# A hybrid S5 and Conformer layer on one core: inputs laid out by the host, and the modulation product in float32

## The chip, the core and the metric

The kernel runs on one core of a Trainium2 chip. The metric is the device time of one execution in microseconds (us). Five engines work beside each other: PE (TensorE, matrix products into PSUM banks), DVE (VectorE), ACT (ScalarE), POOL (GpSimd) and SP (SyncE, which here only issues transfers). Transfers run on 16 DMA engines that all queues share. PE's clock has two levels in the profile, 1.2 and 2.4 GHz, shown as a granted clock of 0.5 and 1.0.

## What is computed

One layer over 2048 latent tokens and 256 context tokens of width 1024, all in float32. The part that the change touches, cut from the reference:

```python
mod_l = silu_c @ ada_w[i] + ada_b[i]           # six vectors of 1024: shift, scale, gate, twice
mod_c = silu_cc @ ada_w[i] + ada_b[i]
nl = modulate(rmsnorm(h_lat, norm1_g[i]), sh1, sc1)    # h * (1 + scale) + shift
nc = modulate(rmsnorm(h_ctx, norm1_g[i]), csh1, csc1)
zl = nl @ w_in[i]                              # 3584 columns: S5 input 512, conv input 1024, gates 2048
zc = nc @ w_in[i][:, :D_S5]
ys_l, _ = s5_mixer(zl[..., :D_S5], zc[..., :D_S5], ...)
```

Behind it come the S5 scans, a Conformer convolution branch, a gated merge, an output product, a gated MLP with a 3x3 convolution, and a last norm. None of that is changed.

## The kernel before

A product of two float32 matrices is made from three reduced products: `split` writes an operand as a high part (cast) and a low part (source minus high part), and `mm3` (lines 487 to 489) issues high by high, high by low and low by high. `gemm` does so for eight slices of 128 rows of the contraction: 24 matmuls into one PSUM bank.

**Order of work.** The Python code gives a program order. A planner puts each engine's instructions in an order of its own from that order, with `urgent()` moving a block 300 places ahead, and hands out buffers. On the chip each engine, and each queue of transfers, runs its list strictly in order.

**Buffers.** Three tags matter: `t16` (six buffers of 16 KB a partition), `z8` (eight of 8 KB) and `raw` (three of 2 KB for weights). PSUM has four banks under `mm` and four under `ax`.

**Phase 1, first part (about 0 to 48 us), `consts` and `ada_first`.** Vectors are loaded as rows and turned into columns on PE (`columns`, line 580). The first 2048 columns of `ada_w` come as eight slabs of 1 MB. Each slab is split (L474, L476 and L478 with tile `slhl`), and PE multiplies both parts by the split, activated condition vectors `sc4` (L662, four columns; 64 matmuls of 512 columns). The result rows go to `adarow` (a `z8` buffer), are turned into columns (L673) and become scale `A1` and shift `S1`.

**Phase 1, second part (about 48 to 207 us), the S5 input `u`.** Tokens are taken in halves of 256 rows, nine in all. For each half: load `x2` with tokens on partitions, squares on ACT (L711), `rstd` (L501 to L506, with a power on POOL), scaling by token (`scaled`, L718), 16 transposes of 128x128 on PE (`turned`, L728) with copies back on ACT (L729), then `modulate`: scale and shift per channel (L737), high part (L739), low part (L741, half of them on POOL). The products with the first 512 columns of `w_in` run per column block `m`: context and the first 512 tokens in pieces of 256 columns, the other blocks in pieces of 512. `u_out` (L746) puts each result into `ub` and stores it (L749). The modulated tokens `nl[0..3]` stay on chip for the rest of `w_in`; `nl[0..2]` are in `t16`, `nl[3]` is four `z8` buffers.

In between, three background pieces run: `s5_params` (loads in small pieces, transposes, about 110 small DVE operations), `taps` and `taps2` (turn the convolution weights, build a banded table and store it to `d_ct`), and `s5_tables` (32 groups; L267, L268 and L271 on POOL, L269, L270 and L272 on DVE, L273 to L275 on ACT, one store each). 24 of the 32 tables are issued before the part ends.

**Phase 2 (about 214 to 892 us).** 88 products of 512 columns for convolution input and gates. After each, `background()` takes three steps of the S5 work in program order: the tables that are left, `s5_ops` (L301 to L345, with L313 to L317 on POOL) and `s5_main` (L371 to L432, one group of five steps at a time, its products at L391, L392 and L407), and steps of the convolution (L895). Everything behind it is dominated by PE.

## Time and profile before

| | us |
|---|---|
| median of 3 runs | 2859.3 |
| lowest and highest | 2857.84, 2859.38 |
| profiled execution | 2868.82 |
| its span, first to last instruction | 2867.0 |

The profile is one execution. Its span leaves 1.8 us of the execution outside. The granted clock is 0.976 over the span. A busy share is time in which an engine had an instruction in work; matmuls are pipelined, so the distance between two starts, not the length of one, is the price of a matmul in a row of many.

### The profile page before, as it was taken

Reading aid. Unit: us, or ns where it says so; the run is one execution under the profiler, and the core shown is the slowest. Engines: PE = TensorE matmul, PEld = TensorE weight load, DVE = VectorE, ACT = ScalarE, POOL = GpSimd, SP = SyncE. Lnnn points to the kernel's source line nnn. Section 1 sums busy time; section 2 is a strip of 40 time slices with the busy share of each in tenths; the row PEclk is TensorE's granted clock in tenths of the full one; section 3 lists DMA queues with packets and bytes.
Section 4 is the critical chain, followed back from the end, with each engine's and each line's share of the span. In section 5 each row is a group of like instructions: output and inputs, shape, how many; then the busy total and the mean of one; then the engine's idle time right before and its main releaser. Section 6 shows DMA issues by size and latency. Waiting matters only on the chain.

```text
span 2867.0 us, 32800 instructions
## 1 busy us (share of the span) xinstructions
PE 2736.4 (95%) x12286; PEld 2233.3 (78%) x12286; DVE 1539.0 (54%) x2363; ACT 840.1 (29%) x1487; POOL 491.1 (17%) x522
## 2 busy tenths in 40 slices
PE   6879999999999999999999999999999989999998
PEld 3767777878787777788888888888888878787887
DVE  7967633333313688666765565565564653414154
ACT  4554421212123544334422122122222222212122
POOL 3446556666610000000000000000000000000000
PEclk8989999999999999999999999999999999999999
DMA  7434635444444666533211111111111144224143
GB/s 254 124 95 149 203 117 161 148 139 148 155 122 137 199 202 191 198 125 132 81 48 46 54 44 48 56 45 44 59 41 48 57 143 135 96 85 133 46 143 102
DMA packets 341421, 326.44 MB, mean 114 GB/s; under 512 B 110306, under 2 KB 255828, under 8 KB 339725
## 3 DMA queue, kind: packets, MB, share of 16 engines
q1 hardware_dynamic: 255101, 225.76, 26.3%
q10 hardware_dynamic: 86160, 98.57, 9.8%
q8 instruction: 97, 1.59, 0.2%
q14 instruction: 63, 0.52, 0.1%
HBM read 221.01 MB, written 103.24 MB: 113 GB/s over the span
## 4 chain that ended last, share of the span: by engine, by line
PE 70%; DVE 11%; DMA 6%; POOL 5%; issue 4%; ACT 3%; SPq 1%; POOLq 0%; ACTq 0%; DVEq 0%
PE ps L487 22%; PE ps L489 22%; PE ps L488 22%; DMA sgab<-d_sg 2%; PE ps L895 1%; PE ps L407 1%; DVE x L737 1%; DVE Hs L430 1%; DMA w_raw<-in_ffn_w_down_dram 1%; DVE tab L269 1%; POOL t L416 1%; POOL t L417 1%; DVE Hs L432 1%; DMA ada<-in_ada_w_dram 0%; POOL t L383 0%
## 5 line engine op out<-in xcount | busy, mean ns | idle before, releaser
L1342 DVE SCALAR_TENSOR_TENSOR acc<-pad,fw,acc 128x1024 f32<-128x1024 f32 x352 | 450.6, 1283 | 238.9 <-ACT acc L1338 229.5
L502 POOL TENSOR_TENSOR rs_y<-rs_v,mhalf 128x1 f32<-128x1 f32 (+1 forms) x41 | 26.2, 638 | 2065.2 <-DVE rs_v L501 2064.9
L487 PE MATMUL ps<-wd,hhl 128*128 128x512 f32 x704 | 276.1, 393 | 16.1 <-ACT hhl L474 9.5
L488 PE MATMUL ps<-wd,hhl 128*128 128x512 f32 x704 | 276.2, 393 | 0.0
L489 PE MATMUL ps<-wd,hhl 128*128 128x512 f32 x704 | 275.6, 392 | 0.0
L430 DVE TENSOR_TENSOR_SCAN Hs<-m,S 64x287 f32<-64x287 f32 x64 | 68.7, 1074 | 245.1 <-POOL S L418 244.5
L478 DVE TENSOR_TENSOR hhl<-hr,hhl 128x512 fp32r<-128x512 f32 (+1 forms) x110 | 63.0, 583 | 246.7 <-ACT hhl L474 246.7
L478 DVE TENSOR_TENSOR w_ch<-w_raw,w_ch 128x512 fp32r<-128x512 f32 x134 | 99.7, 748 | 142.9 <-ACT w_ch L474 142.6
L487 PEld LDWEIGHTS ps<-wd,hhl 128*128 128x128 f32 x704 | 133.5, 190 | 46.2 <-ACT hhl L474 9.9
L474 ACT CAST w_ch<-w_raw 128x512 fp32r<-128x512 f32 x142 | 87.3, 621 | 246.2 <-PE ps L489 165.6
L488 PEld LDWEIGHTS ps<-wd,hhl 128*128 128x128 f32 x704 | 133.4, 190 | 28.7 <-DVE wd L478 1.1
L489 PEld LDWEIGHTS ps<-wd,hhl 128*128 128x128 f32 x704 | 133.5, 190 | 27.9 <-DVE hhl L478 0.2
L474 ACT CAST hhl<-hr 128x512 fp32r<-128x512 f32 (+1 forms) x110 | 57.2, 534 | 267.2 <-PE ps L489 228.3
L487 PE MATMUL ps<-nm0h,w_ch 128*128 128x512 f32 x344 | 133.8, 389 | 0.0
L488 PE MATMUL ps<-nm0l,w_ch 128*128 128x512 f32 x344 | 133.8, 389 | 0.0
L489 PE MATMUL ps<-nm0h,w_ch 128*128 128x512 f32 x344 | 133.8, 389 | 0.0
L487 PE MATMUL ps<-nm1h,w_ch 128*128 128x512 f32 x344 | 133.8, 389 | 0.0
L488 PE MATMUL ps<-nm1l,w_ch 128*128 128x512 f32 x344 | 133.8, 389 | 0.0
L489 PE MATMUL ps<-nm1h,w_ch 128*128 128x512 f32 x344 | 133.8, 389 | 0.0
L487 PE MATMUL ps<-nm2h,w_ch 128*128 128x512 f32 x344 | 133.8, 389 | 0.0
L488 PE MATMUL ps<-nm2l,w_ch 128*128 128x512 f32 x344 | 133.8, 389 | 0.0
L489 PE MATMUL ps<-nm2h,w_ch 128*128 128x512 f32 x344 | 133.8, 389 | 0.0
(409 smaller groups left out, 6538.8 us busy)
## 6 DMA issues: line engine op xcount, KB each, us to landing
w_raw<-in_ffn_w_up_dram SPq DMA_DIRECT2D x88, 256.0 KB
d_hid<-acc ACTq DMA_DIRECT2D x88, 256.0 KB
w_raw<-in_ffn_w_down_dram SPq DMA_DIRECT2D x76, 256.0 KB
grp<-d_rec SPq DMA_DIRECT2D x32, 576.0 KB
hr<-d_hid SPq DMA_DIRECT2D x66, 256.0 KB
d_sg<-sgg ACTq DMA_DIRECT2D x64, 256.0 KB
ada<-in_ada_w_dram SPq DMA_DIRECT2D x64, 256.0 KB
sgab<-d_sg SPq DMA_DIRECT2D x32, 512.0 KB
```

Of the source, the lines that this page charges most:

```text
L269: v.scalar_tensor_tensor(tt, idx, h, tk, op0=OP.mult, op1=OP.subtract)
L407: nc.tensor.matmul(ps[:, :NX], sm[:, i, :], ug, start=True, stop=True)
L416: g_.tensor_tensor(t1, S, tb[:, 0:1, :].to_broadcast([128, 2, NX]), op=OP.mult)
L417: g_.tensor_tensor(t2, S[:, ::-1, :], tb[:, 1:2, :].to_broadcast([128, 2, NX]), op=OP.mult)
L430: v.tensor_tensor_scan(Hs[0:64, i, 1:1 + nsc], mb[0:64], S[0:64, i, 0:nsc], 0.0, op0=OP.mult, op1=OP.add)
L432: v.tensor_tensor_scan(Hs[64:128, i, NX - 1 - nsc:NX - 1][:, ::-1], mb[64:128], S[64:128, i, NX - nsc:NX][:, ::-1], 0.0, op0=OP.mult, op1= ...
L474: self.a.copy(hi, src)
L478: e.tensor_tensor(lo, src, hi.bitcast(F32), op=OP.subtract)
L487: mm(ps, wh, xh, start=first, stop=False)
L488: mm(ps, wh, xl, start=False, stop=False)
L489: mm(ps, wl, xh, start=False, stop=last)
L1342: v.scalar_tensor_tensor(acc[:, h], win(h, t // 3, t % 3), fw[:, i, t:t + 1], acc[:, h], op0=OP.mult, op1=OP.add)
```

## The change

The host hands in further copies of inputs, laid out as the core wants them: `xt` and `ctxt` (tokens with channels on partitions), `cols` (all per-channel vectors as columns), `fdw` and `ct` (the convolution weights, the banded table finished), and the S5 parameters with the state on partitions. `x` and `ctx` in their old form are still loaded, now for the squares alone.

- `columns`, `taps`, `taps2`, `turned`, `scaled` and the transposes in `s5_params` are gone. `xt` is loaded as raw slabs, `xt[b, q]`, two `z8` buffers for each block of 512 tokens.
- `ada_first` multiplies the slabs as they are: 32 matmuls in float32, two columns, no split.
- The reciprocal root of all tokens is collected in `rms`. `row` makes from it a PSUM bank that holds it along the tokens on all partitions: a diagonal matrix on DVE and a float32 product with ones, per 128 tokens.
- Context and block 0 are scaled by token as soon as they are there (`early`) and modulated later (`late`). Blocks 1 to 3 use `modulate`: one DVE operation multiplies by scale and by the token row (read from PSUM), ACT adds the shift and writes the high part, one DVE operation writes the low part. POOL takes a quarter of the low parts in `late`, none in `modulate`.
- The products run by pairs of column blocks with the contraction outermost, in pieces of 512 columns for block 0 too.
- 18 of the 32 tables are issued before the part ends: 3, 6 and 9 behind blocks 1, 2 and 3.

```diff
+        cols = cp.tile([128, NCOL + 32], F32, name="cols")
+        self.dma(cols[:, :NCOL], ins["cols"])
...
         for k in range(8):
-            sl = self.z8("slab", [128, 2048])
-            self.dma(sl, self.ins["ada_w"][128 * k:128 * k + 128, 0:2048])
-            hl = self.t16("slhl", [128, 2, 2048])
-            for h in range(2):
-                hs = slice(1024 * h, 1024 * h + 1024)
+            if k % 2 == 0:
+                sl = self.t16("slab", [128, 2, 2048], F32)
+            self.dma(sl[:, k % 2], self.ins["ada_w"][128 * k:128 * k + 128, 0:2048])
+            for j in range(4):
                 with self.urgent():
-                    self.split(hl[:, 0, hs], hl[:, 1, hs], sl[:, hs], "va"[h], "g" if h and k in (0,2,4) else "v")
-                for i in range(2):
-                    for j in (2 * h, 2 * h + 1):
-                        pe.matmul(acc[j][:4, :], self.sc4[:, k, :], hl[:, i, 512 * j:512 * j + 512],
-                                  start=(k == 0 and i == 0), stop=(k == 7 and i == 1))
+                    pe.matmul(acc[j][:2, :], self.sc[:, k, :], sl[:, k % 2, 512 * j:512 * j + 512],
+                              start=(k == 0), stop=(k == 7))
...
+            def half_stats(i):
                 x2 = self.z8("x2", [128, 2, D])
+                src = ins["x"][256 * i:256 * i + 256, :] if i < 8 else ins["ctx"]
                 self.dma(x2, src.rearrange("(j p) d -> p j d", p=128))
                 ss = small.tile([128, 2], F32, name="nt_ss")
                 for j in range(2):
+                    a.activation(x2[:, j, :], x2[:, j, :], AF.Square, accum_out=ss[:, j:j + 1])
+                self.rstd(small, ss, 2, 1.0 / D, rms[:, 2 * i:2 * i + 2])
+            def row(i, n):
+                ps = psum.tile([128, 512], F32, name="ps", tag="ax")
+                for j in range(n // 128):
+                    dg = small.tile([128, 128], F32, name="dg")
+                    v.tensor_scalar(dg, self.ident, rms[:, 2 * i + j:2 * i + j + 1], None, op0=OP.mult)
+                    self.pe.matmul(ps[:, 128 * j:128 * j + 128], self.ones, dg, start=True, stop=True)
+                return ps
+            def raw_block(b):
+                for q in range(2):
+                    t = self.z8("xt", [128, 4, 512])
+                    self.dma(t, ins["xt"][b][:, 4 * q:4 * q + 4])
+                    xt[b, q] = t
...
+            def modulate(b):
+                nl[b] = self.nl_tiles(b, "nl")
+                for k in range(8):
+                    hi, lo = nl[b](0, k), nl[b](1, k)
+                    w, s1 = xt[b, k // 4][:, k % 4], self.S1[:, 0, k:k + 1]
+                    v.scalar_tensor_tensor(w, w, self.A1[:, 0, k:k + 1], srow[b], op0=OP.mult, op1=OP.mult)
+                    a.activation(hi, w, AF.Identity, bias=s1)
+                    v.scalar_tensor_tensor(lo, w, s1, hi.bitcast(F32), op0=OP.add, op1=OP.subtract)
...
+                if k == 7:
+                    for m in range(2):
+                        wu[m] = self.wtile(ring, w_in, 128 * m)
+                    raw_block(0)
+                    for i in range(2):
+                        half_stats(i)
+                    early([xt[0, q] for q in range(2)], row(0, 512), 512)
...
+            for i in (2, 3):
+                half_stats(i)
+            prepare(1)
+            for i in (4, 5, 6, 7):
+                half_stats(i)
+            u_block(0)
...
+            for b in range(1, 4):
+                if b < 3:
+                    prepare(b + 1)
+                u_block(b)
+                for _ in range((0, 3, 6, 9)[b]):
+                    next(tabs, None)
+            self.dma(self.fw, ins["fdw"])
```

## Rows read from the trace of the kernel before

**Rows 1.** Page, part 1: busy us (share of the span) and instructions of each engine.
```profile
PE 2736.4 (95%) x12286; PEld 2233.3 (78%) x12286; DVE 1539.0 (54%) x2363; ACT 840.1 (29%) x1487; POOL 491.1 (17%) x522
```
**Rows 2.** Windows by stage: length, each engine's busy us (count), granted clock, DMA share, GB/s.
```profile
48.40:207.20 158.80, 134.87 (x740) 116.72 (x740) 121.65 (x313) 87.77 (x178) 72.67 (x89) 0.89 0.44 120
207.20:214.30 7.10, 0.75 (x3) 0.30 (x2) 5.95 (x9) 4.97 (x12) 6.59 (x11) 0.78 0.57 177
214.30:381.00 166.70, 156.50 (x778) 127.17 (x779) 109.04 (x215) 75.05 (x211) 86.93 (x112) 0.97 0.56 172
381.00:800.00 419.00, 401.35 (x1824) 328.60 (x1823) 148.60 (x208) 82.93 (x181) 286.08 (x254) 0.98 0.47 144
800.00:892.00 92.00, 90.81 (x416) 74.75 (x415) 8.20 (x14) 29.36 (x44) 2.05 (x3) 1.00 0.33 102
```
**Rows 3.** Timeline of PE, 41 to 49 us: start, length, what, [idle before, what ended it].
```profile
41.01 2.15 PE L662 MATMUL ps<-slhl,sc 128*4 128x512 f32 x4 [0.35 <-DVE slhl L478]
43.10 1.86 PE L673 MATMUL ps<-ident,adarow 4*128 4x4 f32 x16
48.42 1.01 PE L487 MATMUL ps<-nlch,w_ch 128*128 128x256 f32 x3 [3.46 <-ACT nlch L739]
```
**Rows 4.** Windows around the slabs and the first products, columns as in rows 2.
```profile
2.00:30.00 28.00, 13.75 (x51) 4.87 (x51) 20.03 (x25) 11.05 (x16) 8.46 (x4) 0.94 0.92 363
...
23.40:37.00 13.60, 10.18 (x48) 3.93 (x46) 13.46 (x12) 7.49 (x11) 4.97 (x3) 1.00 0.53 196
37.00:54.00 17.00, 12.28 (x51) 7.82 (x52) 13.18 (x21) 6.66 (x12) 7.72 (x6) 0.50 0.84 272
```
**Rows 5.** Groups of DVE, 0 to 47 us: count, busy us, mean ns, idle before.
```profile
L478 DVE TENSOR_TENSOR slhl<-slab,slhl 128x1024 fp32r<-128x1024 f32 x13 | 17.5, 1379 | 0.2
L476 DVE CAST slhl<-slab 128x1024 fp32r<-128x1024 f32 x8 | 8.8, 1094 | 4.3 <-DMA slab<-in_ada_w_dram 4.3
```
**Rows 6.** Chain that ended last, 360 to 900 us: float32 products, two records each.
```profile
470.90 1.08 PE ps L407 x4
...
493.47 1.34 PE ps L895 x12
```
**Rows 7.** Timeline of PE: first and last of 31 starts, and of 49.
```profile
123.59 0.40 PE L487 MATMUL ps<-nl1h,w_ch 128*128 128x512 f32 x1
...
130.40 0.39 PE L489 MATMUL ps<-nl1h,w_ch 128*128 128x512 f32 x1
...
98.94 0.28 PE L489 MATMUL ps<-nl0h,w_ch 128*128 128x256 f32 x1
...
104.70 0.28 PE L489 MATMUL ps<-nl0h,w_ch 128*128 128x256 f32 x1
```
**Rows 8.** Groups of PE, 48.4 to 207.2 us, columns as in rows 5.
```profile
L728 PE MATMUL ps<-ident,x 128*128 128x128 f32 x128 | 19.7, 301 | 10.0 <-ACT x L729 5.9 <-DVE fw L644 2.3 <-DVE cw L618 1.5
...
L487 PE MATMUL ps<-nl3h,w_ch 128*128 128x512 f32 x32 | 12.9, 421 | 4.8 <-ACT nl3h L739 4.8
```
**Rows 9.** Groups of DVE, 48.4 to 207.2 us.
```profile
L737 DVE TENSOR_SCALAR x<-x,mod 128x256 f32<-128x256 f32 x68 | 30.8, 508 | 8.8 <-ACT x L729 8.8
...
L269 DVE SCALAR_TENSOR_TENSOR tab<-sp,tab 128x320 f32<-128x320 f32 x18 | 12.4, 711 | 8.4 <-POOL tab L268 8.4
...
L741 DVE TENSOR_TENSOR nl3l<-x,nl3h 128x512 fp32r<-128x512 f32 x4 | 2.7, 686 | 7.1 <-DMA d_rec<-tab 6.3 <-ACT nl3h L739 0.8
```
**Rows 10.** Groups of ACT, 48.4 to 207.2 us.
```profile
L711 ACT ACTIVATE nl0h<-x 128x1024 fp32r<-128x1024 f32 x8 | 8.5, 1058 | 0.9 <-ACT x L729 0.9
...
L739 ACT CAST nl2h<-x 128x512 fp32r<-128x512 f32 x8 | 5.0, 621 | 10.0 <-DVE x L737 9.9
```
**Rows 11.** Groups of DVE and of POOL, 214.3 to 381 us.
```profile
L947 DVE TENSOR_TENSOR av<-ps,av 128x512 f32<-128x512 f32 x4 | 2.7, 681 | 6.3 <-PE ps L489 6.3
...
L313 POOL TENSOR_TENSOR ca<-sp,sp 128x288 f32<-128x288 f32 x15 | 12.1, 806 | 41.4 <-PE ps L340 41.4
```
**Rows 12.** Transfers, 10 to 26 us: packets, MB and rate.
```profile
DMA packets 1026, 6.62 MB, mean 413 GB/s; under 512 B 96, under 2 KB 96, under 8 KB 341
```

## What the change will do to the time

> **What bounds the kernel now.** I read the page's busy shares first, then windows cut by stage, then in each stage what PE waits for. PE is busy for 95% of the span [rows 1], so a shorter time means less work on PE, less waiting of PE, or a higher clock. The windows [rows 2] show where there is room. From 214 to 892 us PE is busy 648.7 of 677.7 us at a clock of 0.97 to 1.00. Between 48.4 and 207.2 us, the S5 input, it is busy 134.9 of 158.8 us at a clock of 0.89, with DVE busy 121.7: this stretch is the only long one where PE waits, and part of its busy time is transposes and half-rate matmuls. Before 48.4 us PE does the modulation product, fed by the splitting of slabs: its last four matmuls wait for DVE and end at 43.2 [rows 3], the clock from 37 to 54 us is 0.50 [rows 4], and DVE's splitting is 26.3 us of that time [rows 5]. Everything behind the S5 input starts when that stretch ends, so what the change is worth is read from two stages: 0 to 48.4 and 48.4 to 207.2.
>
> **Part A, the modulation product (0 to 48.4 us).** Removed: the splits and 64 reduced matmuls. Added: 32 float32 matmuls of 512 columns. No row shows one of 512 columns; the nearest are products of 320 columns (two in 1.08 us, so 0.54 each) and of 128 (six in 1.34 us, so 0.223 each) [rows 6]. By columns that is 0.864 or 0.893 us; I take the first, as the wider one is nearer: 27.6 us at 2.4 GHz, 55.3 at 1.2 GHz. The slabs set the other bound. Before, 28 us at 363 GB/s brought 10.2 MB by 30 us [rows 4]. Now 11.6 MB stand ahead of the last slab's landing (eight slabs of 1.05, context twice, 1.1 of S5 parameters); 1.4 MB more at 413 GB/s [rows 12] is 3.4 us, so about 33.5, and its own four matmuls take 3.5: not before 37. With a first slab at about 6 us, 27.6 us of matmuls, some waiting between the early slabs and a few us at the lower clock, the product ends at 37 to 43, I say 41, against 43.2.
>
> What follows is almost as before: 5.3 us from the last matmul to the first context product [rows 3]. But `adarow` is in the tag of eight buffers, and by my count two are S5 parameters, two the context's parts, one the raw context, two the raw slabs of block 0, and the eighth goes to `x2`, which is in use until its squares are done. That `x2` lands after 0.8 MB of weights and 2.1 MB of raw slabs, so about 9.5 us after 33.5 by the same rate, and its squares take 2 x 1.06 [rows 10]: 45. Then the first product starts at 50 or 51. Without the wait it starts at 46. I take 48.4, so **0 us**, with -6 and +3 as ends.
>
> **Part B, the S5 input (158.8 us now).** I build the new stretch from PE's own work, since the inputs to check against it are lighter.
> - Products: a matmul of 512 columns follows the last after 0.227 us (30 steps in 6.81), one of 256 after 0.120 (48 steps in 5.76) [rows 7]. Sixteen products of 24 matmuls at 0.227 are 87.2, four of the context at 0.120 are 11.5: 98.7 us. That block 0 now goes in pieces of 512 gains 192 x 0.120 - 96 x 0.227 = 1.2.
> - Gone: 128 transposes, 19.7 us busy, with 10.0 us of waiting in front of them for copies back and for the weights' turned columns [rows 8].
> - Added: `row`, four float32 matmuls of 128 columns per block at 0.223 [rows 6], with block 0: 3.6 us.
> - The lower clock at the start, 37 to 54 us [rows 4], may well come again: 6 us at half rate, 3 us lost.
> - Waiting. DVE needs two operations per slice, 16 per block, each over 512 elements. The nearest rows are 0.681 with one operand in PSUM [rows 11] and 0.686 without [rows 9]: 11 us per block. ACT's part is eight of about 0.62 [rows 10]. PE needs 24 x 4 x 0.227 = 21.8 per block, so DVE makes a block's input in half the time of the block before, and the pair order lets PE start at the first slice (1.36 us of matmuls for 1.37 us of DVE). Loads per block are 2.1 MB raw and 2.1 MB for squares: 10 us at 413 GB/s [rows 12], inside 21.8. So PE should hardly wait, but block changes cost 4.8 us at the last block now [rows 8], where the buffers of `nl3` came free only when a table was stored [rows 9], and `nl3` still needs four of eight. I put 8 us, ends 3 and 30.
>
> Sum: 98.7 + 3.6 + 3 + 8 = 113.3, against 158.8: **-45.5 us**, ends -50.5 and -23.5.
>
> Who else could be late: DVE over this stretch has 33 us of `modulate`, some 20 for context and block 0, some 12 for roots and diagonals, and 18 tables of three operations at up to 0.711 [rows 9], 38: 103 of 113 us. That fits only because tables give way to the urgent work. ACT has 16 squares of 1.06, 40 high parts and 20 copies out at about 0.6, and 18 tables at three short ones, some 80 us. POOL loses the low parts.
>
> **Part C, behind it.** Six more tables are left for phase 2: 6 x 3 x 0.711 = 12.8 us of DVE and about as much of POOL. They hide in POOL's idle time: it waited 41.4 us in front of L313 [rows 11]. They also take six background steps, 223 instead of 217 by my count, of the 264 that 88 calls give, so no work is pushed out of phase 2. I put 0, ends 0 and +12.8. If that cover is gone, the price is the upper end. The 7.1 us at 207 [rows 2], where the first weights wait for DVE's tables, I leave as they are (-5 to +5). The parameters' transposes, `taps` and the store of the table were hidden or are counted in the waits of B.
>
> **The sum.** 0 - 45.5 + 0 = -45.5. The profiled execution took 2868.8 us with a span of 2867.0, so I expect a span of 2821.5 and an execution of 2823.3. It was 9.5 us (0.3%) above the median of the runs shown; I take the difference off the median: 2859.3 - 45.5 = 2813.8, say **2814 us**.
>
> **What the skill says against it.** The transfers showed 413 GB/s over 16 us [rows 12]. The Trainium skill, "DMA: Bandwidth & Descriptors", section "Bandwidth", has about 358 GB/s of HBM per core bind such loads; the row is above it, so the measurement decides. By the page the 11.6 MB of Part A would take about 1 us longer than I have it, a block's loads 11.7 us instead of 10, still inside 21.8, and the sum would be 2815.
>
> The product's clock was 1.0 from 23.4 to 37 us with PE busy 10.2 of 13.6 us and 0.50 after it, when PE waited for DVE [rows 4]. The Trainium skill, "TensorE: Matmul & The Clock Gate", Part 1, calls the lower level the default and activity what releases it, so a product that waits for slabs could stay low; that is the second rival below.
>
> **Rivals.**
> 1. *Forecast:* PE-bound S5 input, 2801 to 2826.
> 2. *The float32 product stays at 1.2 GHz.* Then it takes 55.3 us from 6 us on and ends at 61 instead of 43.2: +18, so 2814 + 18 = 2832. For it: the dips in rows 4. Against: slabs arrive in about 2.6 us each and take 3.5 at the higher level, so PE is busy without a break once they queue.
> 3. *Transfers are the bound.* `x` comes twice, 8.4 MB more, 20 us at 413 GB/s. If all of it is exposed, 2834. For it: DMA share of 0.84 from 37 to 54 us [rows 4]. Against: 0.44 over the stretch [rows 2], and the many small pieces of parameters are gone.
> 4. *Tables late* (Part C at its upper end): 2814 + 12.8 = 2827.
> 5. *Slower: the eight buffers put loads and products in a row.* `x2`, `xt`, `nl3`, the tables, the parameters and `adarow` share one tag. If a block's loads can start only when the block before has been multiplied, this chain is exposed: two loads of 1.05 MB with squares one after the other, 2 x (2.5 + 2.1), root and row about 4, raw slabs 5.1, first slice 2: 20.3 us per block, for three blocks 61. It decides the sign from 15 us per block (45.5 / 3) on; in full 2814 + 61 = 2875. For it: the 6.3 us wait for a table's store [rows 9]. Against: `nl[1]` and `nl[2]` lie in another tag, and half of the eight are free after the context's products.
> 6. *It does not do what it says:* PE's gain is there but phase 2 is held by S5's own chain and takes it back, 2859. Against: PE is busy 96% there [rows 2], and that chain starts earlier too.
>
> **How the numbers follow.** Chances: forecast 0.55, clock 0.10, transfers 0.16, tables 0.06, buffers 0.05, taken back 0.04, and 0.04 that it is better than forecast (A at -6, gap at -5, B at -50.5: 2797). The likeliest gives 2814. The range takes in the bounds of A, B and C and rivals 2 to 4: 2796 to 2846, leaving out rivals 5 and 6 and a little of the rest. A measurement of this kernel tells about 0.2%, 5.7 us, from no change. Faster 0.91, same 0.04, slower 0.05.
>
> **What would show it.** In the changed profile: the product with the slabs ends near 41 us in steps of about 0.86 us a matmul; no transposes between 48 and 160; PE's product rows 0.227 apart with waits of a few us at block changes; the first product with convolution weights at about 169 instead of 214; and the stretch from there to the end of phase 2 as long as now, 678 us. Wrong would be: product steps of 1.7 us (rival 2), PE waiting for `xt` or `x2` from transfers (3), for buffers (5), or a longer phase 2 (4, 6).

## The result, and the profile after

The changed kernel takes 2810.7 us in the median (four runs, 2806.2 to 2811.9) where the kernel before takes 2859.3 beside it (four runs, 2857.8 to 2863.7): a ratio of 0.9825, 95% interval 0.9808 to 0.9842, or 48.6 us less. The forecast was 2814. The profiled execution of the changed kernel took 2806.2 us with a span of 2804.4, 62.6 us less than the span before. So the two profiled executions differ by 14 us more than the medians do; a second trace of the kernel before (experiment 11) helps to place that.

The page of the changed kernel, part 1, busy us of each engine (to be read beside [rows 1]):

```profile
PE 2711.9 (97%) x12044; PEld 2203.2 (79%) x12044; DVE 1508.0 (54%) x2312; ACT 822.7 (29%) x1446; POOL 459.3 (16%) x504
```

PE is still the engine that is nearly always at work, and of the 62.6 us between the two spans 24.5 are less work of PE. The rest is less waiting of PE. Where it went is read from windows by stage, cut at PE's landmarks (columns as in [rows 2]):

```profile
0.00:41.68 41.68, 31.07 (x65) 5.59 (x65) 17.61 (x111) 7.14 (x14) 7.69 (x16) 0.96 0.96 379
41.68:51.95 10.27, 3.96 (x25) 3.23 (x24) 7.09 (x16) 6.40 (x13) 2.02 (x2) 0.75 0.72 246
51.95:171.21 119.26, 111.39 (x508) 92.08 (x508) 92.47 (x179) 63.21 (x122) 48.52 (x66) 0.94 0.61 184
...
127.00:171.21 44.21, 44.21 (x197) 36.22 (x195) 34.22 (x57) 22.01 (x44) 27.25 (x43) 1.00 0.47 125
171.21:857.20 685.99, 659.44 (x3089) 539.70 (x3088) 287.60 (x461) 207.71 (x466) 381.61 (x381) 0.99 0.50 151
```

The S5 input is 119.3 us long instead of 158.8: 23.5 us less work of PE (111.4 instead of 134.9) and 16.1 less waiting (7.9 instead of 23.9). Its last third has no gap in PE at all. But the stretch between the modulation product and the first context product, 41.7 to 52.0, has PE busy for 4 of 10 us. The landmarks of three traces, each the start of a matmul on PE, with the lengths between them:

| | before | before, second trace | after |
|---|---|---|---|
| first context product | 48.4 | 47.1 | 52.0 |
| first product with convolution weights | 208.5 | 207.6 | 171.9 |
| first product behind phase 2 (sums of `s`) | 908.8 | 906.1 | 857.2 |
| end of the span | 2867.0 | 2860.3 | 2804.4 |
| S5 input, context to convolution weights | 160.0 | 160.5 | 120.0 |
| phase 2, convolution weights to sums | 700.3 | 698.5 | 685.3 |
| behind phase 2 | 1958.2 | 1954.2 | 1947.2 |

Behind phase 2 both kernels have the same code. Over all traces here that part takes 1947 to 1958 us, with traces of either kernel in between, so its 11.0 (or 7.0) us are no part of the change. What is left by the second trace of before is +4.9 - 40.5 - 13.2 = -48.8, close to the difference of the medians.

PE's timeline in the changed kernel (to be read beside [rows 3]):

```profile
6.40 8.68 PE L577 MATMUL ps<-slab,sc 128*2 128x512 f32 x16 [6.40 <-DMA slab<-in_ada_w_dram]
19.22 22.46 PE L577 MATMUL ps<-slab,sc 128*2 128x512 f32 x48 [4.15 <-DMA slab<-in_ada_w_dram]
41.61 0.71 PE L631 MATMUL ps<-dg,ones 128*128 128x128 f32 x4
47.93 0.80 PE L631 MATMUL ps<-dg,ones 128*128 128x128 f32 x2 [5.60 <-DVE dg L630]
48.66 1.86 PE L586 MATMUL ps<-ident,adarow 2*128 2x2 f32 x16
...
51.95 1.01 PE L462 MATMUL ps<-nlch,w_ch 128*128 128x256 f32 x3 [0.71 <-ACT nlch L652]
```

The product ends at 41.7. Its result rows are turned only at 48.66, because PE's list has a `row` matmul of block 0 ahead of those transposes, and that one waits 5.6 us for a diagonal. What DVE and ACT did then:

```profile
42.36 2.35 DVE L644 TENSOR_TENSOR xt<-xt,ps 128x1024 f32<-128x1024 f32 x2 [16.84 <-PE ps L631]
44.63 1.27 DVE L584 COPY adarow<-ps 2x512 f32<-2x512 f32 x2
```

```profile
41.78 1.05 ACT L584 COPY adarow<-ps 2x512 f32<-2x512 f32 x2 [2.71 <-PE ps L577]
```

ACT writes its half of `adarow` at 41.78, 0.1 us behind the product. So the buffer was free, though the squares of block 0 were still to come: the first half's run on ACT from 43.4 to 45.6. DVE's half of `adarow` comes 2.9 us later than ACT's, behind the scaling of the context (L644) in DVE's list. The squares do hold up the transposes, but by another way: the diagonal that PE waits for is made from them, at 47.6.

PE's waits in the S5 input, 51.95 to 171.21 (us in total, times, longest):

```profile
PE ps L631 <- DVE dg L630: 5.9, 4, 2.9
```

Five more waits are each below 0.8 us. PE waits for the diagonals of the token rows and for hardly anything else; no wait for a transfer is among them.

### The profile page after: what moved, and what is told of

Read it like the earlier page. It is cut to its first block, busy times and chain, and to the rows that moved or that the text cites. A ratio compares the mean times of both kernels' runs of the same rounds, so it can differ in the third digit from the quotient of the medians.

```text
span 2804.4 us, 32119 instructions
## 1 busy us (share of the span) xinstructions
PE 2711.9 (97%) x12044; PEld 2203.2 (79%) x12044; DVE 1508.0 (54%) x2312; ACT 822.7 (29%) x1446; POOL 459.3 (16%) x504
## 4 chain that ended last, share of the span: by engine, by line
PE 75%; DVE 9%; DMA 6%; POOL 5%; issue 2%; ACT 2%; SPq 0%; ACTq 0%; POOLq 0%; DVEq 0%
PE ps L464 23%; PE ps L462 23%; PE ps L463 23%; DMA sgab<-d_sg 2%; PE ps L795 1%; DVE Hs L408 1%; PE ps L577 1%; PE ps L385 1%; POOL t L395 1%; DVE Hs L410 1%; DMA slab<-in_ada_w_dram 1%; DMA ada<-in_ada_w_dram 1%; POOL t L394 1%; POOL t L361 1%; PE ps L1112 0%
## 5 line engine op out<-in xcount | busy, mean ns | idle before, releaser
L453 DVE TENSOR_TENSOR w_ch<-w_raw,w_ch 128x512 fp32r<-128x512 f32 x134 | 106.4, 801 | 137.9 <-ACT w_ch L449 137.5
L464 PE MATMUL ps<-nm2h,w_ch 128*128 128x512 f32 x344 | 133.8, 389 | 0.0
L463 PE MATMUL ps<-nm3l,w_ch 128*128 128x512 f32 x344 | 133.8, 389 | 0.0
```

What stands on the lines that cost most here:

```text
L453: e.tensor_tensor(lo, src, hi.bitcast(F32), op=OP.subtract)
L463: mm(ps, wh, xl, start=False, stop=False)
L464: mm(ps, wl, xh, start=False, stop=last)
```

## The experiments

All ratios are to the kernel before, run beside each. Their intervals are 0.001 to 0.002 wide on either side, 3 to 6 us, so two variants of the changed kernel are told apart by their traces more than by their times. "S5 input ends" is the first product with convolution weights. In six kernels nothing ahead of the first context product was changed (5 to 10), and it starts at 53.0 to 54.4 in them, in after at 52.0; so the length from there on is compared, too. The times in the expectations are on a before of 2859.3; the column "time" is the ratio times that.

| kernel | ratio, 95% interval | time | first context product | S5 input ends | between the two | phase 2 |
|---|---|---|---|---|---|---|
| before (second trace) |  |  | 47.1 | 207.6 | 160.5 | 698.5 |
| after | 0.9825, 0.9808 to 0.9842 | 2809.3 | 52.0 | 171.9 | 120.0 | 685.3 |
| 1 float32 product alone | 0.9982, 0.9973 to 0.9991 | 2854.2 | 41.9 | 201.0 | 159.0 | 698.0 |
| 2 other order | 0.9823, 0.9801 to 0.9845 | 2808.7 | 48.8 | 175.7 | 126.9 | 684.4 |
| 3 and late context | 0.9818, 0.9802 to 0.9834 | 2807.3 | 45.5 | 174.3 | 128.8 | 684.3 |
| 4 and stores on SP | 0.9813, 0.9795 to 0.9830 | 2805.8 | 45.5 | 165.8 | 120.4 | 686.8 |
| 5 idle transposes | 0.9850, 0.9834 to 0.9867 | 2816.4 | 54.4 | 180.4 | 126.0 | 684.2 |
| 6 one block at a time | 0.9849, 0.9834 to 0.9864 | 2816.1 | 54.3 | 176.6 | 122.2 | 686.0 |
| 7 fewer loads in rows | 0.9813, 0.9797 to 0.9830 | 2805.8 | 54.1 | 169.3 | 115.2 | 685.1 |
| 8 24 tables | 0.9879, 0.9860 to 0.9899 | 2824.7 | 53.3 | 174.4 | 121.1 | 700.9 |
| 9 23 tables | 0.9865, 0.9851 to 0.9878 | 2820.7 | 53.3 | 175.3 | 122.0 | 691.6 |
| 10 19 tables | 0.9876, 0.9860 to 0.9893 | 2823.8 | 53.0 | 172.5 | 119.5 | 696.9 |
| 12 before with 18 tables | 0.9970, 0.9958 to 0.9982 | 2850.7 | 48.1 | 203.7 | 155.6 | 694.3 |

### 1. The float32 product alone, in the kernel before

```diff
-            hl = self.t16("slhl", [128, 2, 2048])
-            for h in range(2):
-                ... splits, 8 reduced matmuls
+            for j in range(4):
+                with self.urgent():
+                    pe.matmul(acc[j][:2, :], self.sc[:, k, :], sl[:, 512 * j:512 * j + 512],
+                              start=(k == 0), stop=(k == 7))
```

> The kernel before with one part of the change alone: the modulation product in float32 from whole slabs (32 matmuls, no splits); everything else as before. Theory of the prediction: part A is worth nothing, the product is bound by 32 x 0.864 = 27.6 us of matmuls instead of by the splits, so it ends at 41 to 44 us and the first product with context tokens starts at 46 to 50 (48.4 before); time 2859 (2853 to 2862), equal to before. Rival, a gain of its own: 26.3 us of splitting leave DVE, and what waited behind them on DVE comes earlier, so the first context product starts at 43 or 44 and the time is about 2854. Rival, the product stays at 1.2 GHz: steps of 1.7 us, the first context product past 60, time about 2877.

PE's timeline in this kernel:

```profile
6.89 8.70 PE L653 MATMUL ps<-slab,sc 128*2 128x512 f32 x16 [0.61 <-ACT sc L601]
...
16.50 20.76 PE L653 MATMUL ps<-slab,sc 128*2 128x512 f32 x48 [0.67 <-DMA slab<-in_ada_w_dram]
37.19 1.64 PE L717 MATMUL ps<-ident,x 128*128 128x128 f32 x13
38.76 1.15 PE L664 MATMUL ps<-ident,adarow 2*128 2x2 f32 x16
...
41.95 0.50 PE L487 MATMUL ps<-nlch,w_ch 128*128 128x256 f32 x2 [1.56 <-ACT nlch L728]
```

48 records are 24 matmuls, in 20.76 us: 0.865 each. The product ends at 37.3, and the first context product starts at 41.9, 5 to 6.5 us earlier than in the two traces of before. That lead is kept: the S5 input ends at 201.0 instead of 207.6 or 208.5, and the time is 4.6 us less. So the first rival held: the float32 product is worth some 5 us by itself, not nothing. In the changed kernel it is not seen, because there it ends 4.4 us later and is followed by 10.3 us instead of 4.7. The later end comes with the loads in front of the third slab: there PE waits 4.15 us and works at the lower clock behind it (22.46 us for the 24 matmuls), here 0.67. With the context's loads moved behind the fourth slab (experiment 3) it ends at 38.7.

### 2. Another order behind the product

```diff
-                    early([xc[:, 4 * q:4 * q + 4] for q in range(2)], row(8, CTX)[:, :CTX], CTX)
+                    with self.urgent():
+                        early([xc[:, 4 * q:4 * q + 4] for q in range(2)], row(8, CTX)[:, :CTX], CTX)
...
-                    early([xt[0, q] for q in range(2)], row(0, 512), 512)
...
                 late(lambda k: xc[:, k], lambda k: nlc(0, k), lambda k: nlc(1, k), 1)
+            early([xt[0, q] for q in range(2)], row(0, 512), 512)
```

> The changed kernel with another order behind the modulation product, and nothing else: the row and the scaling by token of the context are made while the product still runs, those of block 0 only after the context's modulation has been issued. In the trace of after the product ends at 41.7 us and the first context product starts at 52.0; in between DVE scales the context (2.35 us) ahead of the copies of the result rows, and PE waits 5.6 us for the diagonal of block 0 ahead of their transposes. Theory: the order causes this wait, not a buffer, as the prediction had it; then the first context product starts at 45 to 48, the first product of block 0 at 64 to 68 (70.4), the time is 4 to 6 below after, 2805 to 2807. Rival, a buffer holds the result rows until the squares of block 0 are done at 45.4: the first context product does not start before 49. Rival, block 0 takes it back: its scaling (4.5 us of DVE) now lies behind the context's modulation, so it starts at 70 as before, time 2811.

```profile
25.54 0.49 PE L631 MATMUL ps<-dg,ones 128*128 128x128 f32 x2 [1.78 <-DVE dg L630]
...
28.29 17.96 PE L577 MATMUL ps<-slab,sc 128*2 128x512 f32 x40
46.18 1.16 PE L586 MATMUL ps<-ident,adarow 2*128 2x2 f32 x16
```

Behind the product all went as the theory said: the transposes follow it at once, and the first context product starts 2.6 us behind it instead of 10.3. But the row was now too early in PE's list: PE waited 1.8 us for it inside the product, worked at the lower clock before and behind it, and the product ended at 46.25. The start at 48.8 alone would not refute the buffer, for which not before 49 was said. The order on the engines does: the result rows are written from 44.6 on and turned at 46.2, ahead of the first squares of block 0, which start at 46.8. The first context product came at 48.8, 3.2 us before after's, but PE then waited 3.2 us for a low part of the context on DVE, block 0 started at 71.6 instead of 70.4, block 1 at 105.3 instead of 99.0, and the S5 input ended at 175.7, 3.7 us later than after's. The last rival had decided it: what is gained ahead of block 0 is taken back at block 0 and 1.

### 3. The context's loads behind the fourth slab as well

```diff
-                if k == 1:
+                if k == 3:
                     self.dma(xc, ins["ctxt"])
                     half_stats(8)
+                if k == 6:
                     with self.urgent():
                         early(...)
```

> As the run above, and the context's two loads (2.1 MB) stand behind the fourth slab instead of behind the second. In the trace of after, PE waits 4.2 us for the third slab at 15 us, behind these loads; the kernel before with the float32 product alone ended that product at 37.3 us. Theory: from the first slab on at 6.4 us the product is bound by its matmuls, 27.6 us and some at the lower clock, and ends at 36 to 38; the first context product starts at 41 to 43, the first of block 0 at 60 to 64, where its raw slabs and squares (landed at 43 to 47, squares done at 48.5) are the next to wait for; the time is 8 to 10 below after, 2801 to 2803. Rival, block 0's data are the bound, since 11.6 MB and its own 4.2 MB stand in one queue in either order: block 0 starts where it does in the run above, and the time is equal to that one's.

The product ends at 38.7 and the first context product starts at 45.5 (expected 41 to 43; DVE still scales the context ahead of its copies). The first product of block 0 starts at 70.4, where it does in after, and the S5 input ends at 174.3. The rival held on the time, but not for its reason. ACT and PE in this run:

```profile
74.44 10.56 ACTq L671 DMA_DIRECT2D d_u<-ub x2
85.05 1.06 ACT L622 ACTIVATE x<-x 128x1024 f32<-128x1024 f32 x1 [10.49 <-issue]
```

```profile
88.40 1.22 PE L631 MATMUL ps<-dg,ones 128*128 128x128 f32 x4 [8.55 <-DVE dg L630]
```

ACT takes 10.56 us to issue two stores of the context's result. The squares of block 1 stand behind them in ACT's list, the diagonals wait for the squares, and PE waits 8.55 us for the diagonals.

### 4. The context's stores issued by SP

```diff
             def u_out(ps, n, m, x0s):
+                put = self.store if n == 512 else self.dma
...
-                    self.store(dst, ub[:, :, :nc_])
+                    put(dst, ub[:, :, :nc_])
```

> The run with the late context (product ends at 38.7 us), and the eight stores of the context's S5 input issued by SP instead of ACT. In that run's trace ACT spends 10.6 us from 74.4 on in issuing two of these stores, the squares of block 1 wait behind them, and PE waits 8.6 us for block 1's diagonals; the S5 input ends at 173.6, no earlier than in after (171.2), though its first product starts at 45.5 instead of 52.0. Theory: the issue on ACT is what took the gain back; the squares follow at 70, PE's wait falls to 0 to 2 us, block 1 starts at 94 to 98 (103.8), the S5 input ends at 163 to 168, time 2802 to 2806. Rival, the transfers themselves are the bound (share of the DMA engines 1.0 from 62 to 90 us): SP is held as long as ACT was, the raw slabs of block 1 stand behind the stores and the wait is then for them: 2809 to 2813.

The same two stores issued by SP, and PE's wait for the diagonals of block 1:

```profile
73.63 1.23 SPq L672 DMA_DIRECT2D d_u<-ub  x2
```

```profile
78.03 0.71 PE L631 MATMUL ps<-dg,ones 128*128 128x128 f32 x4 [2.80 <-DVE dg L630]
```

SP needs 1.2 us for the two that had taken ACT 10.6; for the first four the two engines took the same, 2.8 us. PE's wait falls from 8.6 to 2.8 us (0 to 2 was expected), block 1 starts at 97.1 (103.8) and the S5 input ends at 165.8, 8.5 us earlier than in experiment 3 and 6.1 earlier than in after. So the issue on ACT had taken the gain back. Why ACT was held so long there is not shown. The changed kernel has a smaller case of it: two single stores there take ACT 3.5 and 2.6 us. Phase 2 is 1.5 us longer than in after. The ratio, 0.9813, is below that of after, 0.9825, but the intervals overlap widely: by its trace this is the best version, by its time it is not shown to beat the changed kernel.

### 5. Transposes that wait for nothing

```diff
+                if 2 <= i < 8:
+                    for q in range(4):
+                        ps = psum.tile([128, 512], F32, name="pst", tag="ax")
+                        for j in range(4):
+                            self.pe.transpose(ps[:, 128 * j:128 * j + 128], self.ident, self.ident)
```

> The changed kernel with 96 more transposes of 128x128 on PE, 16 for each of the six halves of blocks 1 to 3, from a constant tile into PSUM that nobody reads: they wait for no data and cost no other engine anything. That measures the PE share of the transposes that the change removed. In the trace before, 12 of them in a row took 1.3 us, 0.108 us each. Theory of the prediction, the S5 input is bound by PE: 96 x 0.108 = 10.4 us less what falls into PE's waits of 2.9 and 2.1 us at 78 and 101 us: +6 to +11, time 2817 to 2822. Rival, the stretch is bound by DVE or by transfers and PE has room there: 0 to +3, time 2811 to 2814.

```profile
L628 PE MATMUL pst<-ident x96: 272/273/421, 53.1 to 91.7; 128*128 128x128 f32 x96
```

```profile
54.40:180.38 125.98, 116.60 (x600) 99.62 (x598) 92.99 (x178) 63.43 (x125) 48.49 (x68) 0.97 0.57 169
```

From the first context product on the S5 input takes 126.0 instead of 120.0 us, 6 more, and ends 8.5 later; the ratio is 0.0025 higher, 7 us. That is the price expected of a stretch bound by PE, at the lower end of 6 to 11, and not the 0 to 3 of the rival. DVE, ACT and the transfers had no more to do than in after, so the stretch is not theirs. The rest of the 10.4 us was expected to vanish in PE's waits. That is not what happened: PE's waiting did not shrink (9.4 us, in after 8.6). The granted clock over the stretch is higher instead, 0.97 against 0.94, so that less of PE's work ran at the lower level.

### 6. One column block at a time

```diff
-                for k in range(8):
-                    for ps, m in zip(pss, ms):
+                for ps, m in zip(pss, ms):
+                    for k in range(8):
                         self.mm3(ps[:, :n], wu[m][k], x(k), k == 0, k == 7)
```

> The changed kernel with the column blocks of the S5 input multiplied one after the other, all eight slices of the contraction for one, then for the next, instead of two at a time. Theory of the prediction: with pairs PE needs a new slice every 1.36 us, with single blocks every 0.68 us, and DVE makes one in 1.37; so PE waits where a block's input is made just in time. In the trace that is so for the context and block 0 (52 to 77 us) alone, blocks 1 to 3 are made a block ahead: context 8 x (0.72 to 0.36) and block 0 8 x (1.37 - 0.68) give 3 to 8 us, time 2814 to 2819, and nothing after 99 us changes. Rival, order without effect: what PE waits for in the first column block it would have waited for anyway, as the last slice of block 0 comes at the same time and the weights are all there: 0 to 2 us, time 2811 to 2813. Rival, a loss at each block: 4 x 5.5, time about 2833.

The S5 input ends at 176.6, 4.6 us later, and the ratio is 0.0024 higher, 7 us; but from the first context product on it is only 2.3 us longer (122.2 against 120.0). A loss at each block is ruled out, as block 1's products and those behind it take no longer than in after. Between 3 to 8 for the slices and 0 to 2 for an order without effect the times do not decide. PE's waits speak for the second: for slices, behind the first context product, they are 2.3 us (1.9 for the context, 0.4 for block 0), in after 1.8; what grew are the waits for diagonals, from 5.9 to 8.1. The pairs are worth a few us at most.

### 7. Six loads in rows less

```diff
             def half_stats(i):
+                if 2 <= i < 8:
+                    v.tensor_copy(rms[:, 2 * i:2 * i + 2], rms[:, 0:2])
+                    return
                 x2 = self.z8("x2", [128, 2, D])
```

> The changed kernel without six of the nine loads of tokens in rows: the squares, roots and their loads of tokens 512 to 2047 are left out, and their reciprocal roots are copied from those of the first tokens, so the numbers of blocks 1 to 3 are not the layer's. 6.3 MB less is moved, 15 us at 413 GB/s, and 12 squares leave ACT. Theory of the prediction, the transfers are hidden and squares and roots with them: only the two waits of PE for the diagonals, 2.9 and 2.1 us, and the lower clock behind them go, -3 to -7, time 2804 to 2808. Rival, transfers bound the S5 input: -10 to -15, time 2796 to 2801. Third way, nothing: PE waits for something else at the same places, 2811.

The S5 input from the first context product on:

```profile
54.08:169.20 115.12, 109.95 (x508) 91.94 (x508) 89.72 (x149) 51.63 (x101) 41.97 (x62) 0.93 0.48 130
```

It ends at 169.3, 2.7 us earlier than in after, although 6.3 MB and 12 squares are gone; from the first context product on it takes 115.2 instead of 120.0 us, 4.8 less. The ratio is 0.0012 lower, 3.4 us. So these loads with their squares and roots cost some 3 to 5 us, as the theory had it (3 to 7), not the 10 to 15 of a stretch bound by transfers. Of the two waits that the theory wanted gone only the second went: in front of block 1's diagonals PE still waits 3.3 us, at 77, though neither a load nor a square stands behind them. That wait is no cost of the loads.

### 8 to 12. Where the tables are issued

Phase 2 was the surprise: forecast as long as before, it is 13 to 15 us shorter. Four kernels change only how many of the 32 tables are issued in the S5 input; experiment 11 changes nothing, it is the kernel before, for a second trace.

```diff
-                for _ in range((0, 3, 6, 9)[b]):
+                for _ in range((0, 6, 9, 9)[b]):      # 8; (0, 5, 9, 9) in 9, (0, 3, 7, 9) in 10
```

```diff
-                    for _ in range(2 * (2,2,2,2,2,2)[i - 4]):
+                    for _ in range(2 * (0,1,2,2,2,2)[i - 4]):      # 12, in the kernel before
```

**8, 24 tables.** 

> The changed kernel with 24 instead of 18 of the 32 tables issued in the S5 input (6, 9 and 9 behind blocks 1, 2 and 3), as many as before. Theory of the prediction: the six tables that moved into phase 2 cost nothing there, so moving them back gains nothing; in the S5 input DVE has 27 us free of 119, so they cost nothing there either: 2809 to 2813. Rival (the fourth of the prediction, tables late): phase 2 waits for tables, in the trace of after 7.3 us at 239 us for a table, so -5 to -8, 2803 to 2806. Rival: the tables come ahead of the splitting of the first convolution weights on DVE and the gap at the end of the S5 input, 7.1 us before and 0.7 after, comes back: +4 to +7, 2815 to 2818.

**9, 23 tables.** 

> The changed kernel with 23 tables in the S5 input (5, 9 and 9), five more than in the change and one fewer than in the run with 24. A group of S5 is five steps long and takes one background step each, so five tables more or fewer leave the groups in the same place against the weight tiles, one more or fewer does not. Theory, alignment: phase 2 takes 683 to 688 us as with 18, time 2809 to 2815. Rival, the count: fewer tables left for phase 2 make it longer, by 15.6 us for six; then 697 to 700 for five, time 2822 to 2828.

**10, 19 tables.** 

> The changed kernel with 19 tables in the S5 input (3, 6 and 10 would be the plain count; here 3, 7 and 9), one more than in the change and five fewer than in the run with 24. So far phase 2 took 685.3 us with 18 tables, 691.6 with 23 and 700.9 with 24, and PE waited in it for low parts of weights 8.2, 8.0 and 15.0 us. Theory, alignment: 19 puts the S5 groups where 24 has them, so the waits for low parts are 13 to 17 us and phase 2 takes 691 to 696, time 2817 to 2822 by the before of the prediction. Rival, the count: one table more costs what the others did on average, 1 to 3 us, the waits for low parts stay near 8, phase 2 takes 686 to 688 and the time is 2812 to 2815.

**11, the kernel before again.** 

> The kernel before once more, unchanged, for a second trace of it. The profiled execution of before took 9.5 us more than the median and that of after 4.5 us less; of the 62.6 us between their spans, 42.4 lie ahead of the first convolution product, 9.2 between there and the end of phase 2, and 11.0 behind it, where both kernels have the same code. Theory: the part behind phase 2 differs from run to run; there this trace shows 1947 to 1957 us instead of 1958, and phase 2 loses a few us of its 9.2. Rival: the kernel before really is slower there, by the state in which the S5 input leaves buffers and queues: 1958 again, and 694 for phase 2.

**12, the kernel before with 18 tables.** 

> The kernel before with 18 instead of 24 of the 32 tables issued in the S5 input, as many as in the change: that part of the change alone. So far phase 2, from the first convolution product on, took 700.3 and 698.5 us in the two traces of before, 685.3 in that of after and 700.9 in the changed kernel with 24 tables. Theory: the number of tables alone sets this, since each table left takes one background step and so moves the S5 groups against the weight tiles; with 18 on DVE the low parts of the weights no longer stand behind four scans that wait for POOL. Then phase 2 takes 685 to 688 here as well, PE waits some 8 instead of 20 us for low parts there, and the time is 12 to 16 below before, 2843 to 2849. Rival, the gain in phase 2 needs the host's layouts (no transposes, taps and stores ahead of it): phase 2 stays at 698 to 701, time 2856 to 2862.

PE's waits for the low parts of weights in phase 2, from the views of PE's waits; before:

```profile
PE ps L489 <- DVE w_ch L478: 20.6, 5, 5.1
```

after:

```profile
PE ps L464 <- DVE w_ch L453: 8.2, 4, 3.5
```

24 tables:

```profile
PE ps L464 <- DVE w_ch L453: 15.0, 5, 4.6
```

23 tables:

```profile
PE ps L464 <- DVE w_ch L453: 8.0, 5, 2.3
PE ps L462 <- ACT av L840: 5.9, 1, 5.9
PE ps L318 <- issue: 5.4, 1, 5.4
```

19 tables:

```profile
PE ps L464 <- DVE w_ch L453: 15.6, 4, 5.0
```

before with 18 tables:

```profile
PE ps L487 <- ACT w_ch L474: 13.0, 3, 11.0
PE ps L489 <- DVE w_ch L478: 12.3, 6, 3.5
```

What such a wait looks like on DVE in the kernel before, and then on PE:

```profile
446.31 1.39 DVE L430 TENSOR_TENSOR_SCAN Hs<-m,S 64x287 f32<-64x287 f32 x1 [7.61 <-POOL S L418]
447.71 0.75 DVE L432 TENSOR_TENSOR_SCAN Hs<-m,S 64x287 f32<-64x287 f32 x1
448.48 0.75 DVE L430 TENSOR_TENSOR_SCAN Hs<-m,S 64x287 f32<-64x287 f32 x1
449.24 0.75 DVE L432 TENSOR_TENSOR_SCAN Hs<-m,S 64x287 f32<-64x287 f32 x1
450.02 0.69 DVE L478 TENSOR_TENSOR w_ch<-w_raw,w_ch 128x512 fp32r<-128x512 f32 x1
```

```profile
450.77 0.79 PE L489 MATMUL ps<-nl0h,w_ch 128*128 128x512 f32 x1 [4.65 <-DVE w_ch L478]
451.36 0.63 PE L487 MATMUL ps<-nl0h,w_ch 128*128 128x512 f32 x1
...
454.77 0.63 PE L489 MATMUL ps<-nl0h,w_ch 128*128 128x512 f32 x1
```

DVE's list has the low part of the weights behind four scans of an S5 group. DVE waits 7.6 us for POOL, scans for 3.7, and only then makes the low part; PE stands still for 4.65 us. Then its steps are 0.43 us instead of 0.227 for the rest of that stretch (451.36 to 454.77, eight steps), which costs another 1.6.

Where the groups fall against the weight tiles is set by how many background steps were used up before, one for each table left. (A weight tile is 128 columns of `w_in`, multiplied with the four blocks of tokens; there are 22.) A group is five steps. So 18 and 23 tables should put the groups in the same places, 19 and 24 in others. They do: in the sixteenth weight tile the scans start 0.7, 13.6 and 26.8 us behind the tile's first product with 18 and with 23, 11.6 and 23.6 with 19 and with 24. In all other places the four kernels are alike, so they make a small square:

| phase 2, us | five fewer | five more |
|---|---|---|
| aligned as after | 685.3 (18) | 691.6 (23) |
| one step on | 696.9 (19) | 700.9 (24) |

One step on costs 9 to 12 us, in either column; five more tables in the S5 input cost phase 2 another 4 to 6. How much of it is the groups' is read from the stretch in which they run, from the first product of the sixth weight tile to the end of phase 2 (columns as in [rows 2]); 18, 23, 19 and 24 tables:

```profile
333.00:857.18 524.18, 509.40 (x2344) 417.74 (x2343) 173.34 (x242) 118.59 (x241) 292.73 (x260) 0.99 0.48 145
```

```profile
346.60:866.90 520.30, 505.77 (x2317) 414.04 (x2315) 169.56 (x231) 115.31 (x230) 289.42 (x256) 0.99 0.47 143
```

```profile
337.20:869.47 532.27, 513.11 (x2332) 419.86 (x2332) 163.38 (x235) 116.62 (x233) 288.05 (x256) 0.98 0.46 141
```

```profile
345.90:875.32 529.42, 510.32 (x2317) 417.86 (x2315) 161.81 (x231) 115.22 (x230) 287.84 (x256) 0.98 0.45 138
```

Here one step on costs 8 to 9 us. PE stands still for 14.8 and 14.5 us when aligned, 19.2 and 19.1 one step on, and 34 and 34 steps against 54 and 52 take 0.43 instead of 0.227 us; the two make 4.5 and about 4 us. Of the waits for low parts, those behind scans are 8.2 and 5.4 us against 10.6 and 12.2; the rest of the sums above lies ahead of the groups, behind operations of tables (5.0 us in one wait with 19). So the alignment is shown, at 8 to 9 us.

The count of tables works in the first five weight tiles, where no scan runs yet: they take 161.1 us with 18 and 171.3 with 23, 164.7 with 19 and 171.5 with 24. Of these 7 to 10 us, 3 to 4 come back later: the S5 work is then five steps further on, and PE has 27 and 15 instructions less in the stretch of the groups. What the others are was not separated (with 23, PE waits 5.9 us for a result tile on ACT and 5.4 us for an issue, both there).

No expectation of runs 8 to 10 held in full. Run 8 came out at 2824.7, above all three of its ranges. Run 9 had the alignment right and the time wrong, since it priced the count at nothing. Run 10 had the waits for low parts right (15.6 where 13 to 17 was said), though a third of them is not behind scans, and missed the time by 2 us. In the S5 input itself 23 and 24 tables cost 1 to 2 us (122 and 121 from the first context product on, against 120.0), so there DVE's free time covers them nearly, as the expectation said.

In the kernel before, 18 instead of 24 tables shorten the time by 9.7 us: the S5 input by 4 to 5 (155.6), phase 2 by 4 to 6, to 694.3. The expectation was 685 to 688 and 12 to 16, the rival's 698 to 701: neither held. The groups do move as in the changed kernel, and PE's waits for low parts behind scans fall from 12.3 to 6.8 us. But ahead of the groups nothing is gained: the first five weight tiles take 168.8 us instead of 170.6, where after, with the same 18 tables, takes 161.1. Waits for low parts of 5.4 us stay there, and a new one of 11 us came up, ended at 299, where ACT's list has the high part of a weight tile behind five of the tables that were left: there the tables were not hidden. So the number of tables alone gives about a third of the gain in phase 2. The second trace of before gave 698.5 and 1954.2: phase 2 was not an accident of the first trace, and part of the time behind it was.

## Why the prediction was right, and where it was not

- **What bounds the kernel.** Right. PE is busy 44.2 of 44.2 us from 127 on, and transposes that wait for nothing lengthen the S5 input (experiment 5).
- **Part A, the product.** Its price was right: 0.865 us a matmul (experiment 1) where 0.864 was said, an end at 41.7 where 41 was said, no stay at 1.2 GHz (rival 2). The sum "0 us" was wrong: the first context product starts 3.5 us later than in the profiled execution of before (52.0 against 48.4), just past the bound of +3. The step that failed is the one on `adarow`. The argument by buffers (eight in the tag, the last one held until the squares are done) foretold a start at 50 or 51, which is close to the 52.0 measured, and squares done at 45, which is right (45.6). But that was luck, since no buffer was waited for: ACT wrote into it at 41.78, and in experiment 2 both engines write it ahead of the squares. In its place stand two orders: DVE scales the context ahead of its copies, and PE waits for block 0's diagonal, made from those squares, ahead of the transposes. Alone, the product ends at 37.3 and gains 5 us (experiment 1), inside the end of -6.
- **Part B, the S5 input.** Forecast 113.3 us, measured 119.3. The work was right: the 480 matmuls of the products at 0.227 and 0.120 are 98.7 us, the rows 3.6, and the last 44.2 us hold some 190 matmuls without a gap. The waiting met the number, 7.9 (119.26 - 111.39) where 8 was said, but by luck, as it lies in front of the diagonals and not at block changes or buffers. Mis-sized is the clock: 3 us were put for it, and the steps that are longer than 0.227 and 0.120 add 9.1. Of these, 4.3 lie between 52 and 62 us, behind PE's idle 10 us, 1.8 and 1.6 behind the two longest waits (2.9 us at 77, 2.1 at 101), with steps of 0.43 and 0.21 us, the lower level; 1.4 lie elsewhere. The prediction had only one such piece. Part B was not run alone; if the parts add up, the two that were run alone (4.6 us in experiment 1, 9.7 in 12) leave it 34 of the 48.6 us.
- **Loads inside the products' time (rival 3).** Right: 3 to 5 us are exposed with squares and roots, not 20.
- **Buffers in a row (rival 5).** Not seen; PE waits for no load of a block. A run with a ninth buffer was not made.
- **Part C, tables and phase 2.** Wrong. "0, ends 0 and +12.8" excluded a gain, and phase 2 got 13 to 15 us shorter, counted from the first convolution product. 5.1 of that is the larger part of the gap at 207 [rows 2], left as it was by the forecast: PE waited there for a low part behind DVE's tables, and in after it does not. The step that failed is the count of the six background steps: it asked whether they fit into phase 2, not where they put the S5 groups behind them. By experiments 8 and 10 their number moves phase 2 by 12 to 16 us, of which one step of alignment makes 8 to 9; what makes the rest, ahead of the groups, stays open. Rival 4 had the sign the wrong way round.
- **The sum.** -45.5 was forecast and -48.6 measured, by terms that were off and cancelled: A +3.5 to +4.9 instead of 0, the S5 input with what follows it up to the convolution weights -40 instead of -45.5, phase 2 -13 to -15 instead of 0. So the main term is earned, and that the sum came within 3 us is luck. (The best case in the chances, 2797, adds up to 2798.) Taking the 9.5 us of the profiled execution off was right: the second trace of before has a span of 2860.3.

On the two places of the prediction that draw on the Trainium skill: the changed kernel's transfers from 10 to 26 us ran at this rate (windows, columns as in [rows 2]):

```profile
10.00:26.00 16.00, 11.79 (x24) 1.93 (x23) 13.96 (x83) 3.08 (x7) 0.71 (x1) 0.89 1.01 425
```

The Trainium skill, "DMA: Bandwidth & Descriptors", section "Specifications", gives about 358 GB/s of HBM per core as a limit and 435 GB/s for the fabric; 425 GB/s is above the first and below the second, so here only the second fits.

The product's records show no stay at the lower level once slabs queue, while the waits of 2.9 and 2.1 us in the S5 input are followed by matmuls 0.43 us apart. The Trainium skill, "TensorE: Matmul & The Clock Gate", Part 1, has the lower level as the default that activity releases; both observations agree with that, and it was the price of the second that was set too low.

## What to carry to other kernels

Where engines run their lists in order, taking work away or moving it shifts everything behind it: price a moved step not only by its length but by what then stands in front of the instruction that the bound engine waits for (here weights behind scans, 8 to 9 us for one step of shift). A short wait of PE can cost more than its length: the waits of 2.1 to 4.7 us shown here were followed by matmuls at half pace, which cost another 1.6 to 1.8 us each. Put that into the sum for each such wait. When a part shows no gain inside a larger change, run it alone: the float32 product gave 5 us by itself, and the order that came with the rest took it back.

## What the runs showed that was not expected

- Issuing a store can hold an engine for long: two stores of 128 KB each took ACT 10.56 us (experiment 3), while SP issued the same two in 1.23 us at about the same place (experiment 4).
- Moving six tables of some 2 us of DVE each out of phase 2 made it longer, by 15.6 us (685.3 to 700.9); moving one of them made it longer by 11.6.
- The same code behind phase 2 took between 1947 and 1958 us in the traces of this study.
